# Streamed weights laid out page by page: 8 KB runs per partition instead of 1, 2 or 4 KB

## The chip, the cores and the metric

The kernel runs on one core of a Trainium2 chip. The metric is device time in microseconds (us) from one launch to its end, for the whole program. Lower is better. Laying out the inputs on the host is no part of the time.

## What is computed

Two transformer blocks run one after the other on 256 tokens of width 1024, with 256 context tokens beside them in the first block, in float32. The first block has two layers, the second has one. Every layer has the same shape, cut here to what matters:

```
mod   = silu(c) @ w_ada + b_ada                       # adaLN: w_ada is 1024 x 6144
h     = rms_norm(x) * (1 + scale1) + shift1
x     = x + gate1 * (mixer(h) @ w_out)                # w_out is 1024 x 1024
h2    = rms_norm(x) * (1 + scale2) + shift2
x     = x + gate2 * sum over 2 chosen experts of
          weight * ((silu(h2 @ w_gate[e]) * (h2 @ w_up[e])) @ w_down[e])
```

Layers 0 and 1 choose among 16 experts, whose three matrices are 1024 x 1024 each; layer 0 routes 512 tokens (latent and context), layer 1 routes 256. The third layer, called layer 2 below, chooses among 32 experts with matrices of 1024 x 256, 1024 x 256 and 256 x 1024. An expert's 12 MB (layers 0 and 1) or 3 MB (layer 2) are read from HBM once, so the experts stream 192, 192 and 96 MB.

## The kernel before

**Pages.** All large weights come into SBUF in pages of 1 MB, tiles of the tag `pg` with 8 KB in each of 128 partitions. A page is one DMA issued by SyncE (SP). `page()` takes a source seen as partition x k-tile x column and fetches it in two pages; `wpage()` hands out expert pages from several pools in turn: 8 page buffers in layer 0, 15 in layer 1 and 14 in layer 2. Some of these pools are opened while the mixer before them still runs, so that the first experts' pages are loaded ahead. A load can be issued when the last matmul that reads the old content of its buffer is done.

**Order.** The kernel is written in a tile framework that arranges the instructions on their engines and sets the semaphores; `gather` and `scatter` of other rounds are generators that `s.work()` advances between the matmuls of an expert.

**AdaLN.** `ada_chunk` (L234) multiplies the conditioning vectors with 512 columns of a 1024 x 6144 matrix: two pages, each partition of which holds four rows of 512 columns (2 KB each in HBM). The output projections of the three layers are loaded in the same form.

**Experts of layers 0 and 1.** `expert_wide` (from L1570) goes over the eight k-tiles in steps of two. For each step it loads one page of the gate and one of the up matrix, two k-tiles of 1024 columns each, so that a partition gets two rows of 4 KB that lie 512 KB apart. The matmuls of a k-tile (L1598, L1602) follow, then activation, transposes, and four pages of the down matrix in the same form (L1625, matmuls L1631 and L1635).

**Experts of layer 2.** `expert_narrow` (from L1645) serves two experts of 64 token slots, or four of 32, at a time, in column parts of the PE array. For gate and then up it loads one page an expert, eight rows of 256 columns (1 KB) in a partition (L1658, matmuls L1662), later one page an expert of the down matrix, two rows of 4 KB (L1681, matmuls L1686).

**Which expert.** The experts are visited in an order that depends on how many tokens chose them. `matrices(p)` reads the expert's index from SBUF into a register of SP, and `of_expert` takes a slice of each matrix at that register. `overflow` is a loop for tokens beyond the planned slots, run zero or more times.

**Already packed.** The first layer's input weights (`w0a`, `w0b`, `w0c`), layer 1's `w1` and the third layer's `w2b` are packed by the host, so that a page's partition is one run of 8 KB.

Of the kernel before, what the change touches and what calls it, by code (L numbers as in the profile page):

```python
# [20 lines left out]
P = 128  # L21
D = 1024
KT = 8
# [135 lines left out]
class K:  # L159
# [74 lines left out]
    def ada_chunk(self, ps, which, j, parts):  # L234

        nc, I = self.nc, self.I
        w = I["ada_w"][which] if which < 2 else I["w_ada_2"][0]
        s = 0 if which < 2 else 1
        wt = self.page(w[:, j * 512:(j + 1) * 512].rearrange("(k p) n -> p k n", p=P))
        pa = self.t(ps, [P, 512], "ad", bufs=1) if which == 2 and j >= 4 else self.t(ps, [P, 512], "mm")  # L240
        for kk in range(2):
            for g in range(4):
                k = g + 4 * kk
                nc.tensor.matmul(out=pa[32 * g:32 * g + 32, :], lhsT=self.st[:, s, k, :],
                                 rhs=wt[:, k, :], start=(kk == 0), stop=(kk == 1))
        pt = self.w2(parts, [P, 512]) if which == 2 and j >= 4 else self.t(parts, [P, 512], "part")
        (nc.scalar.copy if j % 2 else nc.vector.tensor_copy)(out=pt, in_=pa)  # L247
        return pt
# [428 lines left out]
    def mixer0(self):  # L677
        tc, nc, I = self.tc, self.nc, self.I
        with ExitStack() as st:
            A = self.pool(st, name="A", bufs=2, reuse_waits="tile")  # L680
            parts = self.pool(st, name="parts", bufs=3, reuse_waits="tile")
            ps = self.pool(st, name="psA", bufs=2, space=PSUM, reuse_waits="tile")
            self.vectors(ps, self.w2(A, [P, NVR, P]))
            x0 = []
            for i in range(4):
                x = self.w4(A, [P, D])
                nc.scalar.dma_start(out=x, in_=I["x" if i < 2 else "ctx"][0, (i % 2) * P:(i % 2 + 1) * P, :])
                x0.append(x)
            self.ada(ps, parts, 0, (1, 0))
            self.gain(0, 1, self.vc[:, V_NM0:V_NM0 + 8])  # L690
            acol, bcol = self.ac[0][:, 1], self.ac[0][:, 0]
            self.lower_bounds()
            hT = tuple(self.t(A, [P, KT, 512], f"hT{i}", F32R, bufs=1) for i in range(2))
            self.h_transposed(ps, A, hT, [(0, 0), (1, 0), (2, 1), (3, 1)], acol, bcol, x0)

            def weights(src):
                return self.split(A, self.page(src), "wh", 3)

            vt, dv = (self.t(A, [P, 4, 512], n, bufs=1) for n in ("vt", "dv"))
            w = weights(I["w0a"][0])  # L700
            self.hm = self.t(A, [P, 8, P], "hm", U8, bufs=1)
            hm = self.w4(A, [P, 1024])
            nc.sync.dma_start(out=hm, in_=I["cst2"][:, D_HM:D_HM + 1024])
            nc.vector.tensor_copy(self.hm.rearrange("p l t -> p (l t)"), hm)
            self.rope_tables(A)
            self.diff_lambda()
            for t in range(4):
                nc.scalar.copy(out=vt[:, t, :], in_=self.proj_tok(ps, hT, t, w, 0, 512))

            yT = Columns(self.xs)  # L710
            hg, df = {}, {}

            def dval(_=0):
                w = weights(I["w0a"][1])
                for t in range(4):
                    nc.scalar.copy(out=dv[:, t, :], in_=self.proj_tok(ps, hT, t, w, 0, 512))

            def H(h):
                if h not in hg:
                    hg[h] = self.hgrn_head(ps, A, hT, weights(I["w0b"][h]), h, vt, yT)  # L720
                next(hg[h])

            def F(h):
                if h not in df:
                    df[h] = self.diff_head(ps, A, hT, weights(I["w0c"][h]), 0, h, dv, yT)
                next(df[h])

            def a0(v):
                self.ada(ps, parts, 0, (v,))

            def a1(v):
                self.ada(ps, parts, 1, (v,))

            for f, v in ((H, 0), (H, 0), (H, 0), (H, 0), (a0, 2), (dval, 0), (F, 0), (F, 0), (H, 1), (F, 0), (H, 1), (H, 1), (H, 1), (a0, 4), (F, 1), (F, 1), (H, 2), (F, 1), (a1, 1), (H, 2), (H, 2), (H, 2), (a0, 3), (F, 2), (F, 2), (H, 3), (F, 2), (H, 3), (H, 3), (H, 3), (a0, 5), (F, 3), (F, 3), (a1, 0), (F, 3), (a1, 2)):
                f(v)
            self.ffn_gain(0)
            self.router_start(ps, A, 0)
            g1 = [self.as_row(ps, "lv", 0, 2, who, self.w4(A, [P, D])) for who in range(2)]
            x0 = []
            for i in range(4):  # L740
                x = self.w4(A, [P, D])
                nc.scalar.dma_start(out=x, in_=I["x" if i < 2 else "ctx"][0, (i % 2) * P:(i % 2 + 1) * P, :])
                x0.append(x)
            wo = []
            for half in range(2):
                w = self.page(I["even_w_out"][0][:, half * 512:(half + 1) * 512].rearrange("(k p) n -> p k n", p=P))
                wo.append(self.split(A, w, ("wh", "vt" if half else "wh"), (3, 1 if half else 3)))
            self.out_proj(ps, A, self.split_y(A, yT, ("hT0", "hT1")), wo, range(4), g1, 0, x0=x0)


    def mixer1(self):
        tc, nc, I = self.tc, self.nc, self.I
        with ExitStack() as st:
# [48 lines left out]
            g1 = [self.as_row(ps, "lv", 1, 2, 0, self.w4(A, [P, D]))]  # L802
            wo = []
            for half in range(2):
                w = self.page(I["w1o"][:, half * 512:(half + 1) * 512].rearrange("(k p) n -> p k n", p=P))
                wo.append(self.split(A, w, "wh", 4))
            self.out_proj(ps, A, self.split_y(Y, yT, ("y0", "y1")), wo, range(2), g1, 1, lambda: self.t(parts, [P, 512], "part"))

# [114 lines left out]
    def mixer2(self):  # L923
        tc, nc, I = self.tc, self.nc, self.I
        self.nw2, self.nw4 = 5, 3
        with ExitStack() as st:
# [55 lines left out]

            def wo():
                half = len(wos)
                w = self.page(I["w_out_2"][0][:, half * 512:(half + 1) * 512].rearrange("(k p) n -> p k n", p=P))
                wos.append(self.split(A, w, ("hT0", "hT1") if half else ("wh", "wh"), 1 if half else 2))

            todo = iter(ada[0:3] + [lru, None, None, *ada[3:4], lru, None, *ada[4:5], lru, *ada[5:], wo, wo])
# [581 lines left out]
    def expert_wide(self, s, src, x64, x32, s0):  # L1570
# [6 lines left out]
        for k2 in range(0, KT, 2):  # L1577
            if s.base is None:
                ws = [self.wpage([P, 2, D]) for _ in range(2)]
                for w, a in zip(ws, src):  # L1580
                    nc.sync.dma_start(out=w, in_=a[k2 * P:(k2 + 2) * P, :].rearrange("(k p) n -> p k n", p=P))
                rows = [[w[:, kk, :] for w in ws] for kk in range(2)]
            s.need(min(k2 + AHEAD, KT))
            for kk in range(2):
# [3 lines left out]
                else:  # L1588

                    w = self.wpage([P, 2, D])  # L1590
                    for i in range(2):
                        nc.sync.dma_start(out=w[:, i, :], in_=src[i][k * P:(k + 1) * P, :])
                    wk = [w[:, i, :] for i in range(2)]
                f = dict(start=(k == 0), stop=(k == KT - 1))
                for w, o in zip(wk, (pg, pu)) if x64 else ():
# [26 lines left out]
        p2 = self.t(ps, [P, 256], "py2", bufs=1) if x32 else None  # L1622
        for k2 in range(0, KT, 2):
            w = self.wpage([P, 2, D])
            nc.sync.dma_start(out=w, in_=src[2][k2 * P:(k2 + 2) * P, :].rearrange("(k p) n -> p k n", p=P))  # L1625
            for kk in range(2):
                g, b = divmod(k2 + kk, 4)
                f = dict(start=(k2 + kk == 0), stop=(k2 + kk == KT - 1))
# [16 lines left out]
    def expert_narrow(self, s, srcs, xT, c0, s0):  # L1645
# [8 lines left out]
        for i in range(2):  # L1654
            ws = []
            for src in srcs:
                w = self.wpage([P, KT, 256])
                nc.sync.dma_start(out=w, in_=src[i].rearrange("(k p) n -> p k n", p=P))  # L1658
                ws.append(w)
            for k in range(KT):  # L1660
                for e in range(ne):
# [16 lines left out]
        wd = []  # L1678
        for src in srcs:
            w = self.wpage([P, 2, D])  # L1680
            nc.sync.dma_start(out=w, in_=src[2].rearrange("(k p) n -> p k n", p=P))  # L1681
            wd.append(w)
        for h in range(2):
            for b in range(2):
# [11 lines left out]
    def moe(self, layer, plan, npages):  # L1696
# [6 lines left out]
        with ExitStack() as st:  # L1703
# [47 lines left out]
            if nt == 4:  # L1751
# [1 line left out]
                nc.vector.tensor_copy(s.ones, self.ones_b)  # L1753
                s.ds = self.t(G, [P, KT], "ds")
                self.tt(s.ds, self.ac[0][:, 3, :, 1], self.ac[0][:, 3, :, 0], ALU.subtract)
            if layer < 2:
                srcs = [I[n][layer] for n in ("moe_w_gate", "moe_w_up", "moe_w_down")]
            else:
                srcs = [I[n][0] for n in ("w_gate_2", "w_up_2", "w_down_2")]

            def matrices(p):

# [95 lines left out]

    @staticmethod
    def of_expert(srcs, e):  # L1860
        return [s_[bass.ds(e, 1)].rearrange("o d n -> (o d) n") for s_ in srcs]

    def overflow(self, s, G, slo, end, nbl, E, ob, srcs, xtile):

# [49 lines left out]
def prepare(inputs):  # L1914
# [16 lines left out]
    def pg(x):  # L1931
        return np.ascontiguousarray(x.transpose(1, 0, 2))

    q, ff, fb, i, g, dq, dk, dv = (w[:, :, j] for j in range(8))
    d["w0a"] = np.stack([pg(i), pg(dv)])
    d["w0b"] = np.stack([pg(np.concatenate([x[:, :, h * P:(h + 1) * P] for x in (q, ff, fb, g)], -1)) for h in range(4)])
    d["w0c"] = np.stack([pg(np.concatenate([x[:, :, h * P:(h + 1) * P] for x in (dq, dk)], -1)) for h in range(4)])
# [2 lines left out]
    w = a["odd_w_qkv"][0]  # L1940
    w = np.concatenate([w[:, :D][:, perm], w[:, D:]], 1).reshape(KT, P, 3, 512)
    d["w1"] = np.ascontiguousarray(w.transpose(2, 1, 0, 3))
    d["w1o"] = np.ascontiguousarray(a["odd_w_out"][0][perm])
    w = a["w_in_2"][0].reshape(KT, P, 1472)
    d["w2a"] = pg(w[:, :, :448])
    d["w2b"] = np.ascontiguousarray(w[:, :, 448:].reshape(KT, P, 2, 512).transpose(2, 1, 0, 3))
# [1 line left out]


_INS = ["x", "ctx", "vecs", "cst", "cst2", "w0a", "w0b", "w0c", "ada_w", "even_w_out", "diff_lambda",  # L1950
        "router_w", "router_b", "moe_w_gate", "moe_w_up", "moe_w_down",
        "final_norm_g", "swa_sink", "w1", "w1o", "w_ada_2", "positions_2", "w2a", "w2b", "q_norm_2", "k_norm_2", "w_q_b_2",
        "w_kv_b_2", "lru_wa_2", "lru_wx_2", "w_out_2", "w_router_group_2", "b_router_group_2", "w_router_expert_2",
        "b_router_expert_2", "w_gate_2", "w_up_2", "w_down_2"]


# [14 lines left out]
```

## Time and profile before

| what | value |
|---|---|
| median of 3 runs | 2214.55 us (2212.21 to 2215.14) |
| the profiled execution | 2221.57 us |
| its span, first to last instruction | 2219.7 us |
| mean granted TensorE clock | 0.962 of full speed |
| TensorE matmul busy | 1978.9 us, 89% of the span |
| VectorE, ScalarE, GpSimd busy | 42%, 25%, 11% |
| read from HBM | 629.51 MB, 284 GB/s over the span |
| loads of SP's and ScalarE's queues | 626.21 MB, 76.0% of the 16 DMA engines' span |

PE is TensorE's matmul, PEld its weight load, DVE VectorE, ACT ScalarE, POOL GpSimd, SPq the queue in which SyncE issues loads. L1598 is line 1598 of the kernel. A busy share is an average over stages with different limits, so it doesn't tell what bounds any one of them. The stages lie in the span about so: layer 0's mixer until 480, its experts until 1050, layer 1's mixer until 1310, its experts until 1780, layer 2's mixer until 1955, its experts until the end. "DMA share" is the summed time of all packets in a stretch over 16 engines' time; it can be a little above 1, since packets overlap.

### The profile page before, as it was taken

The page shows a single profiled execution, that of the slowest core. Times are in us where ns is not written, and L with a number is a line of the kernel's source. Part 1 is how long each engine was busy: PE and PEld are TensorE (multiplying, and loading weights), DVE is VectorE, ACT ScalarE, POOL GpSimd, SP SyncE. Part 2 cuts the span into 40 slices and gives each one's busy share as a digit, 9 for nine tenths or more (in the row PEclk, how much of TensorE's full clock was granted, in tenths as well). Part 3 has the DMA queues.
Part 4 walks back from the last instruction along what each step waited for, and adds up shares of the span by engine and source line. Part 5 has one row for each costly group of instructions (what it writes and reads, how often), then busy time and mean ns, then how long its engine had stood idle before and what let it go on. Part 6 is the DMA issues. An engine that isn't in the chain of part 4 may idle for free. (4 is left out here: it accounts for less than half of the span.)

```text
span 2219.7 us, 29536 instructions
## 1 busy us (share of the span) xinstructions
PE 1978.9 (89%) x11795; PEld 1023.2 (46%) x11795; DVE 940.9 (42%) x2121; ACT 549.9 (25%) x1010; POOL 248.2 (11%) x203
## 2 busy tenths in 40 slices
PE   6999999969999999999699989998877779989976
PEld 3766665755443434343555553332222255655422
DVE  4536546354443425242545543222211156556412
ACT  4333434232111111111433421101000055421100
POOL 0000000120111112031100000000000010113202
PEclk9999999989999999999799999999999989889988
DMA  8423426248999998998354669999999975779997
GB/s 306 157 77 133 146 83 227 76 146 298 346 378 375 360 345 333 351 374 336 105 176 156 237 252 410 409 409 409 409 409 409 410 252 205 267 257 365 360 371 277
DMA packets 238434, 632.58 MB, mean 285 GB/s; under 512 B 15440, under 2 KB 83024, under 8 KB 234960
## 3 DMA queue, kind: packets, MB, share of 16 engines
q1 hardware_dynamic: 236736, 626.21, 76.0%
q10 hardware_dynamic: 1552, 4.39, 0.5%
q8 instruction: 96, 1.57, 0.3%
q14 instruction: 50, 0.41, 0.1%
HBM read 629.51 MB, written 1.05 MB: 284 GB/s over the span
## 5 line engine op out<-in xcount | busy, mean ns | idle before, releaser
L1598 PE MATMUL gu<-pg,xT 128*64 128x512 f32 (+1 forms) x2560 | 489.0, 598 | 27.1 <-DMA pg<-in_moe_w_up_dram 14.6
L1631 PE MATMUL py<-pg,hT 128*64 128x512 f32 (+1 forms) x1280 | 258.5, 597 | 23.6 <-DVE hT L1615 17.4
L1598 PEld LDWEIGHTS gu<-pg,xT 128*64 128x64 f32 (+1 forms) x2560 | 132.5, 124 | 297.9 <-issue 227.7
L1567 POOL TENSOR_TENSOR xs<-xs,t 128x512 f32<-128x512 f32 x110 | 142.3, 1303 | 1121.8 <-DVE t L1222 1121.8
L1546 DVE SCALAR_TENSOR_TENSOR w<-py,swc,w 32x256 fp32r<-32x256 f32 (+3 forms) x142 | 95.5, 673 | 273.0 <-ACT w L1545 270.4
L375 PE MATMUL mm<-hT,wh 128*128 128x512 f32 (+1 forms) x672 | 193.6, 372 | 9.7 <-ACT w L431 5.1
L1545 ACT ACTIVATE w<-py,swc 32x256 fp32r<-32x256 f32 (+3 forms) x142 | 88.3, 622 | 409.7 <-PE py L1631 310.1
L1222 DVE TENSOR_TENSOR hid<-hid,gu 128x512 f32<-128x512 f32 (+2 forms) x52 | 32.8, 631 | 336.7 <-PE gu L1598 272.0
L1222 DVE TENSOR_TENSOR t<-x,w 128x512 f32<-128x512 f32 x156 | 105.7, 689 | 143.9 <-PE x L1563 124.2
L1631 PEld LDWEIGHTS py<-pg,hT 128*64 128x64 f32 (+1 forms) x1280 | 77.0, 124 | 137.4 <-issue 76.2
L375 PEld LDWEIGHTS mm<-hT,wh 128*128 128x128 f32 x672 | 120.3, 194 | 42.5 <-issue 8.9
L1563 PE MATMUL x<-w,S 128*128 128x512 f32 x312 | 112.9, 442 | 22.8 <-DVE t L1222 11.5
L1662 PE MATMUL gu<-pg,xT 128*32 128x256 f32 (+1 forms) x1024 | 109.2, 429 | 22.7 <-DMA pg<-in_w_up_dram 16.8
L375 PE MATMUL mm<-hT,pg 128*128 128x512 f32 (+1 forms) x336 | 124.1, 371 | 0.6 <-DVE pg L356 0.6
L1495 PEld LDWEIGHTS x<-oh,h 128*128 128x128 f32 x704 | 91.6, 189 | 55.8 <-issue 32.0
L1495 PE MATMUL x<-oh,h 128*128 128x256 f32 (+2 forms) x704 | 111.6, 292 | 5.4 <-DVE t L1222 2.4
L1608 ACT ACTIVATE hid<-gu 128x512 f32<-128x512 f32 (+1 forms) x41 | 24.4, 596 | 365.5 <-PE gu L1598 342.2
L1602 PE MATMUL gu<-pg,xT 128*32 128x512 f32 x640 | 111.6, 593 | 0.0
L1498 ACT ACTIVATE xT<-x,ac 128x256 f32<-128x256 f32 (+2 forms) x88 | 48.4, 550 | 211.8 <-PE x L1495 211.7
L1563 PEld LDWEIGHTS x<-w,S 128*128 128x128 f32 x312 | 49.2, 189 | 107.4 <-issue 32.7
L356 DVE TENSOR_TENSOR pg<-pg,wh 128x1024 fp32r<-128x1024 f32 (+1 forms) x74 | 89.0, 1210 | 20.4 <-ACT wh L355 20.3
L366 PE MATMUL mm<-wh,hT 128*128 128x512 f32 (+2 forms) x320 | 95.4, 378 | 2.1 <-ACT part L247 0.7
(500 smaller groups left out, 2621.1 us busy)
## 6 DMA issues: line engine op xcount, KB each, us to landing
pg<-in_moe_w_gate_dram SPq DMA_DIRECT2D x128, 1024.0 KB, 8.8
pg<-in_moe_w_up_dram SPq DMA_DIRECT2D x128, 1024.0 KB, 10.1
pg<-in_moe_w_down_dram SPq DMA_DIRECT2D x128, 1024.0 KB, 9.9
pg<-in_ada_w_dram SPq DMA_DIRECT2D x48, 1024.0 KB, 6.9
pg<-in_w_gate_dram SPq DMA_DIRECT2D x32, 1024.0 KB, 11.4
pg<-in_w_up_dram SPq DMA_DIRECT2D x32, 1024.0 KB, 11.8
pg<-in_w_down_dram SPq DMA_DIRECT2D x32, 1024.0 KB, 11.2
pg<-in_w_ada_dram SPq DMA_DIRECT2D x24, 1024.0 KB, 6.9
```

The source lines that it names most:

```text
L356: nc.vector.tensor_tensor(out=u[:, k:k + m], in0=x[:, k:k + m], in1=t[:, k:k + m].bitcast(F32), op=ALU.subtract)
L366: self.nc.tensor.matmul(out=pm, lhsT=hT[i][:, k, t * P:(t + 1) * P], rhs=w[j][:, k, c0:c0 + n], start=(m == 0), stop=(m == len(ops) - 1))
L375: self.nc.tensor.matmul(out=pm, lhsT=w[i][:, k, c0:c0 + P], rhs=hT[j][:, k, t0:t0 + nt], start=(m == 0), stop=(m == len(ops) - 1))
L1222: self.nc.vector.tensor_tensor(out=out, in0=a, in1=b, op=op)
L1495: nc.tensor.matmul(out=px[:, w, :], lhsT=l_, rhs=r_, start=(i == 0), stop=(i == len(ops) - 1))
L1546: nc.vector.scalar_tensor_tensor(out=lo[o:o + m, c0:c0 + w], in0=x, scalar=wc[o:o + m, :], in1=h.bitcast(F32), op0=ALU.mult, op1=ALU.subtract)
L1563: nc.tensor.matmul(out=px, lhsT=S[0:m, t * P:(t + 1) * P], rhs=y[0:m, cols], start=(i == 0), stop=(i == len(parts) - 1))
L1567: (nc.vector if last and h else nc.gpsimd).tensor_tensor(out=o, in0=o, in1=x, op=ALU.add)
L1598: nc.tensor.matmul(out=o[q:q + m64, :], lhsT=x64[0][:, k, x64[1] + r:x64[1] + r + m64], rhs=w[:, 512 * g:512 * g + 512], **f)
L1602: nc.tensor.matmul(out=pq[32 * q:32 * q + 32, :], lhsT=x32[0][:, k, x32[1]:x32[1] + 32], rhs=wk[q // 2][:, 512 * (q % 2):512 * (q % 2) + 5 ...
L1631: nc.tensor.matmul(out=py[q:q + m64, :], lhsT=h64[:, b, 64 * g + r:64 * g + r + m64], rhs=w[:, kk, 512 * h:512 * h + 512], **f)
L1662: nc.tensor.matmul(out=pg[r * e:r * e + r, 256 * i:256 * i + 256], lhsT=xT[:, k, c0 + r * e:c0 + r * e + r], rhs=ws[e][:, k, :], start=(k ...
```

## The change

The host writes every streamed matrix to HBM in the order in which the pages want it, so that the 8 KB of a partition are one contiguous run. The kernel's loads name the page instead of a strided view. Gate and up of an expert are stacked in one tensor, so that an expert has two source tensors instead of three. Buffers, sizes, the number of pages and all arithmetic stay as they are. In the overflow loop of layers 0 and 1 a page is still fetched in two loads of 4 KB rows.

```diff
@@ ada_chunk
-        w = I["ada_w"][which] if which < 2 else I["w_ada_2"][0]
+        w = I["ada_w"][which] if which < 2 else I["w_ada_2"]
-        wt = self.page(w[:, j * 512:(j + 1) * 512].rearrange("(k p) n -> p k n", p=P))
+        wt = self.page(w[j])
@@ output projections (the same in mixer1 and mixer2)
-                w = self.page(I["even_w_out"][0][:, half * 512:(half + 1) * 512].rearrange("(k p) n -> p k n", p=P))
+                w = self.page(I["even_w_out"][half])
@@ expert_wide
-                for w, a in zip(ws, src):
-                    nc.sync.dma_start(out=w, in_=a[k2 * P:(k2 + 2) * P, :].rearrange("(k p) n -> p k n", p=P))
+                for i, w in enumerate(ws):
+                    nc.sync.dma_start(out=w, in_=src[0][k2 // 2, i])
...
-                        nc.sync.dma_start(out=w[:, i, :], in_=src[i][k * P:(k + 1) * P, :])
+                        nc.sync.dma_start(out=w[:, i, :], in_=src[0][k // 2, i, :, k % 2, :])
...
-            nc.sync.dma_start(out=w, in_=src[2][k2 * P:(k2 + 2) * P, :].rearrange("(k p) n -> p k n", p=P))
+            nc.sync.dma_start(out=w, in_=src[1][k2 // 2])
@@ expert_narrow
-                nc.sync.dma_start(out=w, in_=src[i].rearrange("(k p) n -> p k n", p=P))
+                nc.sync.dma_start(out=w, in_=src[0][i])
...
-            nc.sync.dma_start(out=w, in_=src[2].rearrange("(k p) n -> p k n", p=P))
+            nc.sync.dma_start(out=w, in_=src[1])
@@ of_expert
-        return [s_[bass.ds(e, 1)].rearrange("o d n -> (o d) n") for s_ in srcs]
+        one = {6: "o a m p k n -> (o a) m p k n", 5: "o a p k n -> (o a) p k n", 4: "o p k n -> (o p) k n"}
+        return [s_[bass.ds(e, 1)].rearrange(one[len(s_.shape)]) for s_ in srcs]
@@ prepare, on the host
+    d["ada_w"], d["w_ada_2"] = cols(a["ada_w"], 512), cols(a["w_ada_2"][0], 512)
+    d["even_w_out"], d["w_out_2"] = cols(a["even_w_out"][0], 512), cols(a["w_out_2"][0], 512)
+    d["moe_gu"] = np.stack([pairs(a["moe_w_gate"]), pairs(a["moe_w_up"])], 3)
+    d["moe_d"] = np.ascontiguousarray(pairs(a["moe_w_down"]))
+    d["moe2_gu"] = np.stack([a[n][0].reshape(32, KT, P, 256).transpose(0, 2, 1, 3) for n in ("w_gate_2", "w_up_2")], 1)
+    d["moe2_d"] = np.ascontiguousarray(a["w_down_2"][0].reshape(32, 2, P, D).transpose(0, 2, 1, 3))
...
-    d["w1o"] = np.ascontiguousarray(a["odd_w_out"][0][perm])
+    d["w1o"] = cols(a["odd_w_out"][0][perm], 512)
```

`cols(x, n)` puts a matrix's column blocks of n in front, then partition, k-tile and column; `pairs(x)` puts pairs of k-tiles in front, then partition, the two k-tiles and the columns.

## Rows read from the trace of the kernel before

**Rows 1.** The page: busy shares, GB/s in 40 equal slices, DMA packets.

```profile
PE 1978.9 (89%) x11795; PEld 1023.2 (46%) x11795; DVE 940.9 (42%) x2121; ACT 549.9 (25%) x1010; POOL 248.2 (11%) x203
...
GB/s 306 157 77 133 146 83 227 76 146 298 346 378 375 360 345 333 351 374 336 105 176 156 237 252 410 409 409 409 409 409 409 410 252 205 267 257 365 360 371 277
DMA packets 238434, 632.58 MB, mean 285 GB/s; under 512 B 15440, under 2 KB 83024, under 8 KB 234960
```

**Rows 2.** Busy time by stretches; the first line names the columns.

```profile
core 0: us, PE busy (x) PEld busy (x) DVE busy (x) ACT busy (x) POOL busy (x), PEclk, DMA share, GB/s
10.00:30.00 20.00, 13.76 (x68) 3.17 (x68) 5.97 (x19) 4.42 (x9) 1.65 (x3) 1.00 1.05 388
30.00:35.00 5.00, 2.66 (x20) 1.43 (x20) 0.51 (x3) 1.33 (x3) 0.00 (x0) 1.00 1.04 427
31.00:35.00 4.00, 2.66 (x20) 1.43 (x20) 0.51 (x3) 1.33 (x3) 0.00 (x0) 1.00 1.01 422
540.00:1040.00 500.00, 487.37 (x3690) 195.05 (x3690) 199.82 (x361) 80.58 (x142) 92.75 (x71) 1.00 0.95 362
1344.00:1776.00 432.00, 367.81 (x1616) 118.38 (x1614) 86.76 (x159) 34.53 (x54) 36.26 (x28) 1.00 1.03 409
1957.00:2046.00 89.00, 88.60 (x608) 52.75 (x609) 45.66 (x122) 17.93 (x31) 17.79 (x14) 1.00 0.95 322
2046.00:2204.00 158.00, 128.66 (x956) 54.80 (x956) 53.94 (x108) 15.44 (x27) 32.19 (x25) 0.91 1.05 365
2046.00:2100.00 54.00, 50.92 (x417) 25.34 (x414) 29.26 (x61) 8.62 (x15) 16.73 (x13) 1.00 1.07 365
2100.00:2204.00 104.00, 77.73 (x541) 29.46 (x543) 24.68 (x47) 6.82 (x12) 15.47 (x13) 0.87 1.04 364
```

**Rows 3.** PE's waits, 0 to 45: us in total, times, longest.

```profile
PE mm L244 <- DMA pg<-in_ada_w_dram: 10.6, 6, 6.2
```

**Rows 4.** PE's waits for loads, 1490 to 1790.

```profile
PE gu L1598 <- DMA pg<-in_moe_w_up_dram: 14.6, 24, 0.6
PE gu L1598 <- DMA pg<-in_moe_w_gate_dram: 12.5, 21, 0.7
...
PE py L1631 <- DMA pg<-in_moe_w_down_dram: 5.5, 7, 1.9
```

**Rows 5.** PE's waits for loads, 2100 to 2205.

```profile
PE gu L1662 <- DMA pg<-in_w_up_dram: 16.8, 9, 2.5
PE gu L1662 <- DMA pg<-in_w_gate_dram: 5.9, 4, 2.4
PE py L1686 <- DMA pg<-in_w_down_dram: 1.4, 2, 0.7
```

**Rows 6.** PE's waits, 540 to 1040: the longest entry.

```profile
PE py L1631 <- DVE hT L1615: 5.4, 7, 0.8
```

**Rows 7.** SP's issues in time, 1386 to 1402: start, duration, load.

```profile
1391.85 2.45 SPq L1581 DMA_DIRECT2D pg<-in_moe_w_up_dram  x1
...
1396.98 2.31 SPq L1581 DMA_DIRECT2D pg<-in_moe_w_up_dram  x1
```

**Rows 8.** SP's issues in time, 572 to 592.

```profile
584.54 0.37 SPq L1581 DMA_DIRECT2D pg<-in_moe_w_gate_dram  x1
```

**Rows 9.** The page's list of loads: count, KB each, median us to landing.

```profile
pg<-in_moe_w_gate_dram SPq DMA_DIRECT2D x128, 1024.0 KB, 8.8
...
pg<-in_w_gate_dram SPq DMA_DIRECT2D x32, 1024.0 KB, 11.4
...
pg<-in_w0a_dram SPq DMA_DIRECT2D x4, 1024.0 KB, 8.5
```

**Rows 10.** SP's issues in time, 1254 to 1260.5.

```profile
1254.73 0.37 SPq L1581 DMA_DIRECT2D pg<-in_moe_w_gate_dram  x1
1259.16 0.37 SPq L1625 DMA_DIRECT2D pg<-in_moe_w_down_dram  x1
1259.58 0.50 SPq L1581 DMA_DIRECT2D pg<-in_moe_w_up_dram  x1
```

More of the change, by code (lines that the diff above doesn't have):

```diff
@@ L804, in mixer1 @@
             for half in range(2):
-                w = self.page(I["w1o"][:, half * 512:(half + 1) * 512].rearrange("(k p) n -> p k n", p=P))
+                w = self.page(I["w1o"][half])
                 wo.append(self.split(A, w, "wh", 4))
@@ L984, in wo @@
                 half = len(wos)
-                w = self.page(I["w_out_2"][0][:, half * 512:(half + 1) * 512].rearrange("(k p) n -> p k n", p=P))
+                w = self.page(I["w_out_2"][half])
                 wos.append(self.split(A, w, ("hT0", "hT1") if half else ("wh", "wh"), 1 if half else 2))
@@ L1755, in moe @@
                 self.tt(s.ds, self.ac[0][:, 3, :, 1], self.ac[0][:, 3, :, 0], ALU.subtract)
[L1756 to L1759, printed above, removed]
+            srcs = [I[n][layer] for n in ("moe_gu", "moe_d")] if layer < 2 else [I[n] for n in ("moe2_gu", "moe2_d")]
             def matrices(p):
@@ L1934, in prepare, with cols, pairs @@
     q, ff, fb, i, g, dq, dk, dv = (w[:, :, j] for j in range(8))
+    def cols(x, n):
+        x = x.reshape(*x.shape[:-2], KT, P, x.shape[-1] // n, n)
+        return np.ascontiguousarray(np.moveaxis(x, (-2, -3, -4), (-4, -3, -2)))
+    def pairs(x):
+        x = x.reshape(*x.shape[:-2], x.shape[-2] // (2 * P), 2, P, x.shape[-1])
+        return np.moveaxis(x, -2, -3)
+    d["ada_w"], d["w_ada_2"] = cols(a["ada_w"], 512), cols(a["w_ada_2"][0], 512)
[4 more added lines that the diff above has]
+    d["moe2_d"] = np.ascontiguousarray(a["w_down_2"][0].reshape(32, 2, P, D).transpose(0, 2, 1, 3))
     d["w0a"] = np.stack([pg(i), pg(dv)])
@@ L1950 @@
 _INS = ["x", "ctx", "vecs", "cst", "cst2", "w0a", "w0b", "w0c", "ada_w", "even_w_out", "diff_lambda",
-        "router_w", "router_b", "moe_w_gate", "moe_w_up", "moe_w_down",
+        "router_w", "router_b", "moe_gu", "moe_d",
         "final_norm_g", "swa_sink", "w1", "w1o", "w_ada_2", "positions_2", "w2a", "w2b", "q_norm_2", "k_norm_2", "w_q_b_2",
         "w_kv_b_2", "lru_wa_2", "lru_wx_2", "w_out_2", "w_router_group_2", "b_router_group_2", "w_router_expert_2",
-        "b_router_expert_2", "w_gate_2", "w_up_2", "w_down_2"]
+        "b_router_expert_2", "moe2_gu", "moe2_d"]
 def kernel(**inputs):
```

## Prediction

> **What bounds the kernel now.** I read the page first, then stretches of it, then PE's waits, then the queue that issues the loads. On the page TensorE (PE) is busy for 89% of the span, so the kernel looks PE-bound as a whole; but the row of GB/s is not level, and one run of eight slices stands at 409 to 410 without a break [rows 1]. A stream that holds one value for 444 us (eight slices of 55.5 us) is at its own limit, whatever the average says. So the question is asked stage by stage [rows 2]:
>
> - Start, 10 to 30: DMA share 1.05 and 388 GB/s, PE busy 13.8 of 20 us. These are layer 0's adaLN weights, in runs of 2 KB. The stream bounds.
> - Layer 0's experts, 540 to 1040: PE 487.4 of 500 us. PE bounds.
> - Layer 1's experts, 1344 to 1776: 409 GB/s, PE 367.8 of 432 us. The stream bounds.
> - Layer 2's experts: until 2046 PE 88.6 of 89 us, then 128.7 of 158 us at 365 GB/s. First PE bounds, then the stream.
>
> PE's waits say the same from the other side. It waits for adaLN pages for 10.6 us within the first 45 us [rows 3], for layer 1's pages for 14.6 + 12.5 + 5.5 = 32.6 us, all after 1490 [rows 4], and for layer 2's for 16.8 + 5.9 + 1.4 = 24.1 us, all after 2100 [rows 5]. The list over the whole span holds no other wait of PE for a load than the small vectors at the start. In layer 0's list no load appears at all; the longest entry is 5.4 us on VectorE [rows 6].
>
> The issuing queue tells full from starved. In layer 1 one issue after the other takes 2.3 to 2.5 us: the queue behind it is full, and that is about the time of one 1 MB page at 409 GB/s (2.56 us) [rows 7]. In layer 0 an issue takes 0.37 us and comes when PE gives a page free [rows 8].
>
> **The change part by part.**
>
> *Number of loads.* Every page stays 1 MB and keeps its one issue, on SP, into the same buffer: as many issues as before, of 1024 KB each [rows 9]. Bytes are unchanged. No engine gets or loses an instruction. SP works out two run-time base addresses an expert instead of three; SP is not on the path (it waits for PE or for the queue), so I take nothing. The overflow loop, the only place where a page still comes in two loads of 4 KB runs, isn't entered: the 128 gate pages are 32 experts at 4 each [rows 9]. The host's rearranging is outside the time.
>
> *Run length.* This is all there is. A partition's 8 KB now come from one run instead of two of 4 KB (layers 0 and 1, layer 2's down matrices), four of 2 KB (adaLN and output projections), or eight of 1 KB (layer 2's gate and up). What a run length is worth is read from saturated stretches of this trace: 365 GB/s where two thirds of the bytes come in 1 KB runs, 388 at 2 KB, 409 at 4 KB [rows 2]. The packed weights of the first layer are already in 8 KB runs (the w0a row of [rows 9]), and the one stretch in which they alone fill the queues, 31 to 35 us, shows 422 GB/s at a share of 1.01 [rows 2]. It is short, and a few smaller packets are in it. So I take 422, with 409 (the longer run brings nothing over 4 KB) and 427 (the same pages with the us before them, 30 to 35) as bounds.
>
> *Start.* 20 us at 388 become 20 x 388/422 = 18.4: 1.6 us, since PE waits there and everything follows from these vectors. Bounds 1.0 and 1.8.
>
> *Layer 0 experts and the mixers.* Nothing. The work that hides the loads is PE's own: 487.4 busy of 500 us, and the idle 12.6 are waits on VectorE and ScalarE [rows 2, 6]. Were that cover gone, layer 0's stream would be the end, and it too would be faster than before.
>
> *Layer 1 experts.* 432 x (1 - 409/422) = 13.3 us. It needs waits of PE that can go: 32.6 us are there, so the stream stays the bound and PE goes on waiting, some 19 us. That PE's waits begin only at 1490 while the queue is full from about 1344 does not halve this: in between PE eats up pages loaded ahead, and a faster stream makes that stock last longer. Bounds 0 and 432 x (1 - 409/427) = 18.2.
>
> *Layer 2 experts.* 158 x (1 - 365/422) = 21.3 us, against 24.1 us of waits that can go: nearly all of PE's waiting, so PE and the stream would end almost together. Bounds 158 x (1 - 365/409) = 17.0 and, PE allowing no more, 24.1. The granted clock of 0.87 after 2100 [rows 2] should rise towards 1.00 as the gaps close; I take nothing for it, because the stream then sets the end.
>
> *Sum.* 1.6 + 13.3 + 21.3 = 36.2 us. The profiled execution took 2221.57 us (span 2219.7, 1.9 around it), which is 7.0 above the median of the runs. Without the 36.2 it is 2185.4, and the median goes from 2214.55 to 2178.4 us.
>
> [...]
>
> **The rivals.**
>
> 1. *4 KB is already the top.* The stream gains in layer 2 and at the start, not in layer 1: 17.0 + 1.0 = 18.0 us, 2196.5 us. For it: the 422 rests on 4 us of trace. Against it: those 4 us have a share of 1.01, so they aren't flattered by an idle queue.
> 2. *PE takes over early in layer 2.* From 2046 to 2100 PE is busy 50.9 of 54 us [rows 2]; if pages that come sooner find no free buffer there, only the stretch from 2100 counts: 104 x (1 - 364/422) = 14.3 in place of 21.3, in all 29.2, 2185.3 us. Against it: the queue is full there (share 1.07), so buffers are being given free in time.
> 3. *The runs don't become long.* The experts are addressed by a number known only at run time; if such a load were still cut into its inner rows, layers 1 and 2 would keep 4 KB and 1 KB packets, and a ceiling that run length doesn't move gives the same. 2214.6 us, or 1.6 less for the start. For it: no load with a run-time address in this trace has a whole-page run to show. Against: in memory such a page is as contiguous as w0a's, whose address is fixed.
> 4. *Slower: another order of instructions.* The order on the queues isn't that of the code: a down page of layer 1 goes out between a gate and an up page, which the code issues after all of these [rows 10]. So the order is arranged when the program is built, and cheaper loads may change it. The place where it would hurt is layer 0, where PE has no slack. The price: to end over 2219 it must eat the 36.2 and 4.4 us more, 40.6 over 16 experts, a new wait of 2.5 us in each, which is three times the 0.8 us of the longest single wait on VectorE in layer 0's list now [rows 6]. Below that point the change is still faster.
>
> **How the numbers follow.** Forecast 0.65; rival 1 0.12; rival 2 0.13; rival 3 0.05; rival 4 0.05. I give the forecast that much because both halves of it, the present rate and the future one, are read from the same trace, and PE's waits are large enough to pay it. The time is that of the forecast, 2178 us. Its upper rate gives 1.8 + 18.2 + 24.1 = 44.1 us, 2170.4; rival 1 gives 2196.5. The range from 2170 to 2196 holds the forecast, rival 2 and about half of rival 1, some 0.84; it leaves out rivals 3 and 4. What a measurement of this kernel can tell from no change is 0.2%, 4.4 us. Faster by more than that: 0.65 + 0.12 + 0.13 = 0.90. Within it: rival 3, 0.05. Slower: rival 4, 0.05.
>
> **What would show each step.** The packets: 480 expert pages, 72 of adaLN and 12 of output projections make 564 x 128 = 72,192 packets of 8 KB, in place of 215,040 smaller ones (384 x 256 + 64 x 1024 + 32 x 256 + 84 x 512); the total falls from 238,434 [rows 1] to about 95,600. If it stays near 200,000, rival 3 holds. Layer 1's level row of GB/s should read about 422 instead of 409 and be 13 us shorter; 409 again is rival 1. PE's waits for layer 1's loads should fall from 32.6 to about 19 us, layer 2's from 24.1 to about 3. Layer 0's stretch should keep its length within 2 us; if it is longer by tens of us, with waits that aren't in the old list, rival 4 holds. I am wrong if the gain lies outside these three stretches, or if pages arrive sooner and the end doesn't move.

## The result and the profile after

The changed kernel takes 2178.23 us (median of 4 runs, 2176.03 to 2183.1), against 2214.85 us for the kernel before, run beside it: a ratio of 0.9838 [0.9823, 0.9852], so 36.6 us faster, with an interval of 32.8 to 39.2. The prediction was 2178 us. The profiled execution took 2183.1 us, its span 2181.3.

The page of the changed kernel, as in [rows 1]; the last two lines are from its list of loads, as in [rows 9]:

```profile
PE 1961.6 (90%) x11795; PEld 1018.2 (47%) x11795; DVE 941.4 (43%) x2121; ACT 550.1 (25%) x1010; POOL 247.1 (11%) x203
...
GB/s 315 153 80 135 145 87 232 78 116 289 348 377 374 369 363 346 316 362 404 126 150 172 177 258 367 421 421 420 421 421 421 421 283 239 253 243 376 397 420 303
...
DMA packets 95586, 632.58 MB, mean 290 GB/s; under 512 B 15440, under 2 KB 17488, under 8 KB 19920
...
pg<-in_moe_gu_dram SPq DMA_DIRECT2D x320, 1024.0 KB, 9.3
pg<-in_moe_d_dram SPq DMA_DIRECT2D x160, 1024.0 KB, 9.8
```

Instructions, loads and bytes are as many as before; the packets fell from 238,434 to 95,586. The level run of slices, 409 to 410 before, is at 420 to 421; it fills seven slices of 54.5 us, where it filled eight of 55.5. (Layer 2's pages are counted with the others: 256 + 64 and 128 + 32.)

The stretches of [rows 2], moved by what the kernel had gained up to each:

```profile
core 0: us, PE busy (x) PEld busy (x) DVE busy (x) ACT busy (x) POOL busy (x), PEclk, DMA share, GB/s
10.00:30.00 20.00, 12.13 (x68) 3.06 (x68) 6.39 (x21) 6.16 (x12) 2.21 (x4) 1.00 1.02 422
537.00:1037.00 500.00, 487.35 (x3692) 195.17 (x3690) 199.80 (x361) 80.41 (x141) 92.71 (x72) 1.00 0.93 362
1341.00:1761.00 420.00, 366.16 (x1618) 119.86 (x1616) 87.03 (x159) 34.62 (x55) 36.23 (x28) 1.00 1.01 421
1939.00:2028.00 89.00, 88.60 (x606) 52.82 (x608) 45.75 (x122) 18.10 (x32) 17.77 (x14) 1.00 0.87 337
2028.00:2166.00 138.00, 120.22 (x962) 53.20 (x961) 53.94 (x109) 15.44 (x27) 32.44 (x25) 0.95 0.99 408
2028.00:2081.00 53.00, 50.07 (x418) 24.67 (x415) 29.20 (x62) 8.62 (x15) 16.42 (x13) 1.00 1.00 407
2081.00:2166.00 85.00, 70.15 (x546) 28.53 (x547) 24.74 (x47) 6.82 (x12) 16.02 (x13) 0.92 0.98 408
```

Layer 0's stretch holds the same work in the same 500 us. Layer 1's stretch does the same matmuls (1,616 and 1,618 are counted) in 420 instead of 432 us, layer 2's second stretch (956 and 962) in 138 instead of 158. The last two lines cut that stretch where [rows 2] cut it at 2100: 53 instead of 54 us come before the cut, 85 instead of 104 behind it. So 19 of the 20 us are won at the end, though the stream is faster (407 instead of 365 GB/s) from the start: until the cut PE is the bound, and what comes sooner is kept in the buffers and spent later.

PE's waits for loads in layer 1 (1480 to 1790), as in [rows 4]:

```profile
PE gu L1598 <- DMA pg<-in_moe_gu_dram: 18.6, 34, 0.7
...
PE py L1631 <- DMA pg<-in_moe_d_dram: 3.9, 7, 1.5
```

in layer 2 (2080 to 2180), as in [rows 5]:

```profile
PE gu L1662 <- DMA pg<-in_moe_gu_dram: 11.0, 7, 1.9
PE py L1686 <- DMA pg<-in_moe_d_dram: 1.8, 3, 0.6
```

and at the start (0 to 45), as in [rows 3]:

```profile
PE mm L244 <- DMA pg<-in_ada_w_dram: 8.1, 5, 2.5
```

32.6 us became 22.5 in layer 1, 24.1 became 12.8 in layer 2, 10.6 became 8.1 at the start.

Where each layer's experts begin and end can be read to a tenth of a us: from the start of the layer's first routing matmul (L1345) to the start of its last scatter matmul (L1563), and in layer 2 to the end of the last instruction that counts as busy, 5 us before the end of the span. A mixer is what lies between. In us, from the profiled executions (four of the experiments told below have columns as well):

| stage | before | after | layer 0 alone | layer 1 alone | layer 2 alone | adaLN alone |
|---|---|---|---|---|---|---|
| mixer 0, with the start | 472.9 | 469.7 | 468.6 | 465.7 | 468.7 | 467.9 |
| experts 0 | 592.6 | 592.9 | 592.8 | 593.4 | 593.5 | 592.7 |
| mixer 1 | 237.6 | 237.7 | 237.2 | 237.7 | 237.6 | 238.1 |
| experts 1 | 479.3 | 467.1 | 478.5 | 466.7 | 478.6 | 478.8 |
| mixer 2 | 167.1 | 164.3 | 164.2 | 161.5 | 164.0 | 162.6 |
| experts 2 | 265.2 | 244.5 | 265.1 | 265.1 | 245.7 | 265.1 |

The experts' stages repeat within 1.2 us in this table wherever their layout is the same. Mixers 0 and 2 don't: they wander over 7 and 6 us in kernels that leave them untouched, with the same matmuls in the same order, and their granted clock lies below 1 (0.95 before and 0.96 after in the last 290 us of mixer 0). In the twelve profiled executions of whole kernels mixer 2's length goes with that clock: 166.8 to 167.1 us at a mean of 0.87, 162.7 to 164.3 at 0.88 to 0.89, 161.4 to 162.6 at 0.90. What one profiled execution gains there says nothing of the change.

### The profile page after: what moved, and what is told of

It is laid out like the page before. It is cut to its first block, busy times and chain, and to the rows that moved or that the text cites. A ratio compares the mean times of both kernels' runs of the same rounds, so it can differ in the third digit from the quotient of the medians.

```text
span 2181.3 us, 29536 instructions
## 1 busy us (share of the span) xinstructions
PE 1961.6 (90%) x11795; PEld 1018.2 (47%) x11795; DVE 941.4 (43%) x2121; ACT 550.1 (25%) x1010; POOL 247.1 (11%) x203
## 2 busy tenths in 40 slices
DMA packets 95586, 632.58 MB, mean 290 GB/s; under 512 B 15440, under 2 KB 17488, under 8 KB 19920
## 5 line engine op out<-in xcount | busy, mean ns | idle before, releaser
L375 PE MATMUL mm<-hT,wh 128*128 128x512 f32 (+1 forms) x672 | 189.1, 365 | 10.0 <-ACT w L431 5.1
L1222 DVE TENSOR_TENSOR hid<-hid,gu 128x512 f32<-128x512 f32 (+2 forms) x52 | 32.8, 632 | 306.5 <-PE gu L1598 261.7
L1563 PE MATMUL x<-w,S 128*128 128x512 f32 x312 | 114.9, 450 | 21.3 <-DVE t L1222 10.1
L1662 PE MATMUL gu<-pg,xT 128*32 128x256 f32 (+1 forms) x1024 | 101.2, 401 | 11.0 <-DMA pg<-in_moe_gu_dram 11.0
L1563 PEld LDWEIGHTS x<-w,S 128*128 128x128 f32 x312 | 50.4, 192 | 106.5 <-issue 31.7
```

The source lines that it names most:

```text
L375: self.nc.tensor.matmul(out=pm, lhsT=w[i][:, k, c0:c0 + P], rhs=hT[j][:, k, t0:t0 + nt], start=(m == 0), stop=(m == len(ops) - 1))
L1222: self.nc.vector.tensor_tensor(out=out, in0=a, in1=b, op=op)
L1563: nc.tensor.matmul(out=px, lhsT=S[0:m, t * P:(t + 1) * P], rhs=y[0:m, cols], start=(i == 0), stop=(i == len(parts) - 1))
L1662: nc.tensor.matmul(out=pg[r * e:r * e + r, 256 * i:256 * i + 256], lhsT=xT[:, k, c0 + r * e:c0 + r * e + r], rhs=ws[e][:, k, :], start=(k ...
```

## The experiments

**Each part alone.** Four kernels put one part of the new layout into the kernel before. Each edit is the part of the change's diff that bears on its layer; layers left alone keep the old views:

```diff
-                srcs = [I[n][layer] for n in ("moe_w_gate", "moe_w_up", "moe_w_down")]
...
+                srcs = [I["gu1"], I["d1"]]
...
-                    nc.sync.dma_start(out=w, in_=a[k2 * P:(k2 + 2) * P, :].rearrange("(k p) n -> p k n", p=P))
...
+                    nc.sync.dma_start(out=w, in_=src[0][k2 // 2, i] if len(src) == 2 else
+                                      src[i][k2 * P:(k2 + 2) * P, :].rearrange("(k p) n -> p k n", p=P))
```

(layer 1; for layers 0 and 2 the same with their tensors; for adaLN and the output projections only the edits in `ada_chunk` and the mixers).

> Only layer 0's experts are packed in 8 KB runs; all else as before. My theory (run length sets the rate of the stream, and the time follows only where PE waits for it): no change beyond 2 us, about 2214.8 us, because PE has no wait for a load in that stretch. Rival (faster loads help wherever there are loads, for instance through fewer packets beside PE's own reads): a third to two fifths of the gain, 13 us or more, since these are 192 of the 564 MB repacked.

Measured: 2215.72 us, ratio 1.0003 [0.9992, 1.0013], experts 0 592.8 us against 592.6. The packets fell to 213,858 and the time stood still: layer 0's loads are covered.

> Only layer 1's experts are packed. My theory: 432 us at 409 GB/s become 432 x 409/421, 12.3 us less, about 2202.5 us, with PE's waits for layer 1's loads down from 32.6 to about 22 us. Rival (the gain of layer 1 depends on what came before or after it): clearly less than 10 or more than 15 us.

Measured: 2200.22 us, 0.9936 [0.9921, 0.995]; experts 1 12.6 us shorter, the level at 420 to 421 GB/s. PE's waits for layer 1's loads in this kernel (1470 to 1780):

```profile
PE gu L1599 <- DMA pg<-in_gu_dram: 19.0, 34, 1.0
...
PE py L1633 <- DMA pg<-in_d_dram: 3.4, 7, 1.3
```

That is 22.4 us, against 22.5 in the whole change. Rival 1, that 4 KB is already the top, falls here.

> Only layer 2's experts are packed. My theory: 158 us at 365 GB/s become 158 x 365/421, 21 us less, about 2194 us. Rival (PE is the bound until 2100 and only the rest counts): 14 us less, 2201 us.

Measured: 2191.5 us, 0.9889 [0.9874, 0.9903]; experts 2 19.5 us shorter. That is far nearer the forecast's 21.3 than rival 2's 14.3. As shown above for the whole change, the stretch from 2046 to 2100 gains hardly any time itself; the pages that come sooner in it find free buffers, and the time is won after it.

> Only the adaLN weights and the output projections are packed. My theory: 1.5 us at the start and nothing elsewhere, about 2213.3 us. Rival (the mixers gain from earlier pages as well, as the two traces seem to say: 1.7 us in layer 0's mixer and 2.4 in layer 2's): 5.6 us less, 2209 us. If the rival is wrong, those 4 us come from the granted clock, which differs from run to run.

Measured: 2212.61 us, 0.9996 [0.9983, 1.0009]: a gain of 1.5 us can't be seen in totals. The 5.6 us of the rival, a ratio of 0.9975, lie outside the interval, so the shorter mixers of the first pair can't all be the change's doing. The 1.5 us can be seen in the trace. The first transposing matmul of L327 comes when the first adaLN vectors are there; its line in the kernel before, and after it in this one (the last numbers are first and last start):

```profile
L327 PE MATMUL tp<-cst,w x80: 271/421/478, 33.6 to 1798.3; 128*128 128x128 f32 x80
```

```profile
L327 PE MATMUL tp<-cst,w x80: 271/421/477, 31.6 to 1793.4; 128*128 128x128 f32 x80
```

In the four kernels with 2 KB adaLN runs (before and the three experiments above) it starts at 33.6 to 34.0 us, in the changed kernel, this one and the six further variants of the changed kernel at 31.6 to 32.1. The two groups don't touch.

The four ratios add up to -1.76%, 39 us, against 36.6 for the whole: the parts are additive within their intervals.

**The loads by themselves.** This kernel streams weights in six run lengths, one after the other:

```diff
+            for j in range(4):
+                nc.sync.dma_start(out=part(w, j, 2048).rearrange("p (k n) -> p k n", n=256), in_=mb(g, 4 * i + j, 1).rearrange("(k p n) -> p k n", p=P, n=256))
...
+            for j in range(4):
+                nc.sync.dma_start(out=part(w, j, 2048), in_=mb(g, 4 * i + j, 1).rearrange("(p n) -> p n", p=P))
...
+            nc.sync.dma_start(out=w, in_=mb(u, 4 * i, 4).rearrange("(p n) -> p n", p=P))
```

> Leaves out all of the computation: it only loads 24 MB each in runs of 1, 2, 4, 8 and 16 KB and 8 MB in runs of 32 KB, from contiguous pages, one after the other, with full queues, and returns no result of the model. My theory: a packet costs a fixed time and its bytes at one rate, so with 4 KB at 409 and 1 KB at about 349 GB/s the fixed part is about 9.5 ns and the rate 27.35 bytes per ns and engine: 349, 389, 411, 424, 431 and 434 GB/s. Rival (8 KB is the end of it): 16 and 32 KB stay at 421 to 424. Second rival (the rates in the kernel are set by what runs beside the loads): 1, 2 and 4 KB are well above 350, 389 and 411 when nothing else runs.

Its stretches of 1, 2, 4, 8, 16 and 32 KB, in this order:

```profile
core 0: us, DVE busy (x) POOL busy (x), PEclk, DMA share, GB/s
20.00:60.00 40.00, 2.00 (x13) 0.00 (x0) 1.00 1.10 348
90.00:130.00 40.00, 2.15 (x14) 0.00 (x0) 1.00 1.05 387
150.00:190.00 40.00, 2.40 (x16) 0.00 (x0) 1.00 1.03 410
210.00:245.00 35.00, 2.21 (x15) 0.00 (x0) 1.00 1.01 422
265.00:300.00 35.00, 1.50 (x14) 0.00 (x0) 1.00 1.00 427
320.00:330.00 10.00, 0.21 (x2) 0.00 (x0) 1.00 1.00 431
```

388, 409 and 422, which the prediction read between other work, come back within 1 GB/s on an idle core. So what runs beside the loads doesn't set the level (the second rival), and run length does: from 1 to 8 KB a load is 1 MB throughout. The rates go on rising, to 427 and 431, so the first rival falls too, though the loads of 16 and 32 KB runs are also larger (2 and 4 MB) and the last line rests on 10 us. All six are within 4 GB/s of what was expected. Every megabyte lies contiguous in HBM here, as layer 1's and layer 2's pages did before: that doesn't help as long as a partition's share of it is cut up.

**A run length given back.** The changed kernel, with layer 2's gate and up pages in four runs of 2 KB:

```diff
-                nc.sync.dma_start(out=w, in_=src[0][i])
+                nc.sync.dma_start(out=w.rearrange("p (a k) n -> p a (k n)", a=4), in_=src[0][i].rearrange("a p k n -> p a (k n)"))
...
```

> The changed kernel, but layer 2's gate and up pages come in 2 KB runs (four in a partition); each page is still one contiguous megabyte. My theory: the 57.7 MB from 2046 on go at 2/3 of 389 and 1/3 of 421, about 399 GB/s, in 144.5 in place of 137 us: 7 us slower than the changed kernel, about 2185.5 us. Rival (that a page is packed and contiguous counts, not the run): as the changed kernel, 2178 us.

Measured: 2184.08 us, 0.9868 [0.9845, 0.989]; experts 2 250.1 us, 5.6 longer than in the changed kernel (244.5), where 7 were expected. The two kernels differ in the 64 x 128 x 3 = 24,576 packets that are added (120,163 in all) and in nothing else.

**Only the place in HBM.** Layer 1's 8 KB runs stay, but lie 64 KB (gate and up) or 32 KB (down) apart instead of one behind the other:

```diff
-                    nc.sync.dma_start(out=w, in_=src[0][k2 // 2, i])
+                    nc.sync.dma_start(out=w, in_=src[0][:, k2 // 2, i] if s.layer == 1 else src[0][k2 // 2, i])
...
+    d["moe_gu1"] = np.ascontiguousarray(gu[1].transpose(0, 3, 1, 2, 4, 5))
+    d["moe_d1"] = np.ascontiguousarray(dn[1].transpose(0, 2, 1, 3, 4))
```

> The changed kernel, but layer 1's 8 KB runs of one page lie 64 KB apart (down matrix 32 KB) instead of one behind the other. My theory: the run is what counts, so the time stays at 2178 us within 3 us, 421 GB/s in layer 1. Rival (the gain came from a page being one contiguous megabyte): layer 1 falls back to 409 or below, 2190 us or more. The pages of before were contiguous as well in the experts, which speaks against the rival already.

Measured: 2183.6 us, 0.9849 [0.9828, 0.9871]; experts 1 467.2 us against 467.1, the level at 420 to 421. At these distances the pages needn't be contiguous. (The median is 5 us above that of the changed kernel, and the intervals of the two ratios overlap. In the profiled execution, at 2188.85 us the slowest of the four, the part that was changed has none of the excess; mixers 0 and 2 took 471.7 and 167.0 us, the upper end of their wander.)

**Longer runs still.** Layer 1's gate and up as one load of 2 MB in 16 KB runs, with the same 15 MB of buffers (four of 2 MB, seven of 1 MB):

```diff
-                ws = [self.wpage([P, 2, D]) for _ in range(2)]
-                for i, w in enumerate(ws):
-                    nc.sync.dma_start(out=w, in_=src[0][k2 // 2, i])
+                if self.pairs:
+                    w = self.wpair()
+                    nc.sync.dma_start(out=w, in_=src[0][k2 // 2])
+                    ws = [w[:, 0], w[:, 1]]
...
```

> The changed kernel, but in layer 1 a gate and an up page are one load of 2 MB with 16 KB runs, in 4 buffers of 2 MB and 7 of 1 MB instead of 15 of 1 MB. My theory: two thirds of the bytes at about 429 and a third at 421, 426 GB/s instead of 421: 417 us become 412, 5 us less than the changed kernel, about 2173 us. Rival (coarser buffers make PE wait): no gain or a loss, 2178 us or more.

Measured: 2187.24 us, 0.9877 [0.9859, 0.9896]; experts 1 471.1 us, 4.0 longer than in the changed kernel; where the rest of the 9 us between the medians lies isn't shown. The rate did rise, to 424 to 427. But at the start of the stage, where PE eats what was loaded ahead, the queue runs dry. Two stretches of this kernel:

```profile
core 0: us, PE busy (x) PEld busy (x) DVE busy (x) ACT busy (x) POOL busy (x), PEclk, DMA share, GB/s
1320.00:1340.00 20.00, 20.00 (x104) 9.06 (x102) 5.17 (x14) 3.59 (x7) 0.00 (x0) 1.00 0.82 347
1340.00:1360.00 20.00, 20.00 (x94) 6.66 (x92) 5.79 (x16) 1.97 (x4) 0.00 (x0) 1.00 0.87 340
```

and the same of the changed kernel, whose stage begins 1.5 us later:

```profile
1320.00:1340.00 20.00, 20.00 (x103) 8.75 (x99) 5.76 (x15) 4.39 (x8) 0.00 (x0) 1.00 0.98 399
1340.00:1360.00 20.00, 20.00 (x93) 7.13 (x94) 7.10 (x21) 2.91 (x5) 0.00 (x0) 1.00 1.01 420
```

In these 40 us 20 x (52 + 80) KB/us = 2.6 MB fewer came in, 6.3 us at 420 GB/s. The higher rate wins back less than half of that (from 1440 to 1700 it is 425 instead of 421 GB/s, 2.4 us). A buffer of 2 MB comes free only when its last k-tile is used, and it is for such a buffer that SP waits before it issues, in the same 40 us of this kernel and of the changed one:

```profile
SPq L1581 <- PE gu L1603: 29.9, 6, 12.7
```

```profile
SPq L1581 <- PE gu L1598: 14.6, 6, 5.1
```

The variant also ties gate and up to 8 MB of the buffers and down to 7, where any page could take any buffer before; no run tells this from the size of the buffers. No variant here beats the changed kernel.

**How good layer 0's cover is.** The changed kernel with layer 0's pages in shorter runs, of 1 KB and of 2 KB (then n=512):

```diff
+                    if s.layer == 0:
+                        nc.sync.dma_start(out=w.rearrange("p a (b n) -> p (a b) n", n=256), in_=src[0][k2 // 2, i].rearrange("a p n -> p a n"))
...
```

> The changed kernel, but layer 0's pages come in 1 KB runs. My theory: layer 0 draws 362 GB/s and PE bounds it; 1 KB runs give 348 at most, so the stream becomes the bound there: 500 x 362/348 = 520, up to 20 us more in layer 0's stretch, with new waits of PE for loads in it; 2193 to 2198 us. Rival (layer 0 is covered whatever the loads do): no change, 2178 us.

Measured: 2191.15 us, 0.9895 [0.9879, 0.9912]; experts 0 604.5 us, 11.6 longer. The page's row of GB/s, whose slices 11 to 19 now stand level:

```profile
GB/s 314 154 78 135 144 88 230 78 140 293 348 348 348 348 347 348 347 347 348 191 154 162 184 269 356 422 421 420 421 421 421 422 277 240 235 246 378 401 420 299
```

Two waits of PE for loads are new (467 to 1071, where the changed kernel's list has none):

```profile
PE py L1641 <- DMA pg<-in_moe_d_dram: 1.7, 1, 1.7
PE gu L1605 <- DMA pg<-in_moe_gu_dram: 1.5, 7, 0.2
```

They make 3.2 of the 11.6 us. Another 8.8 show as busy time: PE's in the stage went from 571.45 to 580.22 us, with equal counts and a granted clock of 0.99 in both. The weight loads (PEld) tell more. They have waits for pages of layer 0 as well, where the changed kernel's list for the stage has none:

```profile
PEld gu L1605 <- DMA pg<-in_moe_gu_dram: 12.1, 18, 1.2
PEld py L1641 <- DMA pg<-in_moe_d_dram: 3.1, 2, 2.5
```

These 15.2 us are enough for the 11.6. In this stage PE is busy for 580.22 and PEld for 240.28 of 604.5 us, so weight loads and matmuls overlap, and part of such a wait can lie under matmuls that still count as busy. That the 8.8 us come from there fits these numbers, but no line shows it.

> The changed kernel, but layer 0's pages come in 2 KB runs. My theory: 387 GB/s are still more than the 362 that PE takes, so layer 0's stretch keeps its length within 2 us and PE gets no wait for a load; 2178 us. Rival (the cover thins gradually, because PE's demand comes in bursts): 3 to 10 us more.

Measured: 2179.64 us, 0.9851 [0.9834, 0.9867]; experts 0 592.6 us. PE's and PEld's lists for the stage have no wait for a load. At 387 GB/s the cover is whole, at 348 it is not; PE draws 362 there.

**Layer 1 below the old level.** The changed kernel with layer 1 in 2 KB runs, by the same edit with `s.layer == 1` and n=512:

> The changed kernel, but layer 1's pages come in 2 KB runs. My theory: 177 MB at 387 instead of 421 GB/s take 457 instead of 420 us: 37 us more in layer 1's stretch, 2215 us, which is 24 us more there than with the 4 KB runs of before. Rival (the stretch has a second bound near 409): less than 15 us more.

Measured: 2217.57 us, 1.0018 [1.0002, 1.0034]; experts 1 505.3 us, 38.2 longer than in the changed kernel and 26.0 longer than before. The level is 386 to 387, and PE's waits for layer 1's loads over the whole span are

```profile
PE gu L1605 <- DMA pg<-in_moe_gu_dram: 41.6, 57, 1.0
...
PE py L1641 <- DMA pg<-in_moe_d_dram: 10.2, 19, 1.6
```

51.8 us against 22.5. One layer's run length, two steps shorter, eats up the whole change.

## Why the prediction was right, step by step

- **Start: 1.6 forecast, 1.5 measured** (33.6 to 32.1 in the profiled pair, 1.5 to 2.4 between the two groups of kernels). Over the whole span PE's waits for adaLN pages only fell from 10.6 to 9.8 us in the profiled pair, and the totals can't tell 1.5 us, so that these reach the end isn't shown.
- **Layer 0 and the mixers: 0 forecast, 0 shown.** The experts' stage is 0.3 us longer, and alone it gave 1.0003. The named cover is what hides it, PE's own work, which draws less than the stream can give: 1 KB runs, which give less than PE draws (348 against 362 GB/s), cost 11.6 us.
- **Layer 1: 13.3 forecast, 12.2 measured** (479.3 to 467.1 us; 12.6 alone). The term is off by its rate: the level is 421, not the 422 of the short w0a stretch, and 432 x (1 - 409/421) = 12.3. The waits kept 22.5 us, not 19: 10.1 us of waiting went, and PE's busy time over the stretch fell by 1.7 us as well.
- **Layer 2: 21.3 forecast, 20.7 measured** (19.5 alone). The mechanism held, but that the size comes so near is partly luck. The stretch ran at 408 GB/s, not 422, and by that rate the term is 158 x (1 - 365/408) = 16.7 us. The other 3.3 of its 20.0 us were won ahead of it: over the 89 us before, the stream brought 337 GB/s instead of 322 [rows 2], 1.3 MB that no longer had to come. One sentence was wrong: that nearly all of PE's waiting would go. 12.8 us stayed, because PE's own work got shorter: over the second stretch it was busy 120.2 instead of 128.7 us, at a granted clock of 0.95 instead of 0.91 [rows 2]. 8.4 us less work and 11.3 us less waiting make 19.7 of the 20.0 by which the stretch shrank. The clock rose as the prediction said, and the gain isn't larger for it since the stream sets the end. Rival 2 was right that PE is the bound until 2100, and wrong that the faster stream is lost there: 19 us, not 14.3, were won after it.
- **The sum: 36.2 forecast, 36.6 measured** in medians. The stages of the profiled pair give 1.5 + 12.2 + 20.7 = 34.4; the profiled execution's own 38.5 has about 4 us of the mixers' wander in it. So that forecast and medians meet within 0.4 us is luck; what the record bears is some 34 us from the named stages, and an interval of 32.8 to 39.2 for the whole.
- **Rival 3** fell with the packets, 95,586 against 95,600 foretold: a page addressed by a register is cut in 8 KB packets as one with a fixed address is (packets of 8 KB or more went from 238,434 - 234,960 = 3,474 to 95,586 - 19,920 = 75,666: 72,192 more, 128 for each of the 480 expert pages and of the 84 with fixed addresses). **Rival 4** fell too: the instructions of PE, ScalarE and GpSimd and SP's loads stand in the same order as before, VectorE's but for two pairs of neighbours that swapped.
- **A ceiling that run length doesn't move**, the other half of rival 3, isn't borne out: with nothing else on the core 1 KB runs reach 348 GB/s and 8 KB runs 422, and the 1 KB layout cost 11.6 us in layer 0.

## What to carry to other kernels

Look for slices of the GB/s row that stand level: in this kernel the stream was at the limit of its run length there, and a longer run was worth length x (1 - old rate / new rate), 12.3 us by the sum and 12.2 by the trace in layer 1. A stretch in which PE still bounds isn't lost for this: the pages that come sooner wait in free buffers and pay later, as in layer 2, where 19 of the 20 us were won behind it. Where PE bounds, compare what it draws with the rate of the run length; layer 0's 362 GB/s were safe at 387 and not at 348. Longer runs were worth having here until they needed coarser buffers: 16 KB runs won 3 to 6 GB/s, and the stage was 4 us longer for a queue that ran dry.

## What the runs showed that I had not expected

**A fixed price per packet.** The prediction read each rate by itself; the loads alone put them on one line. If every run is one packet (for 1 to 8 KB the packet counts of the two kernels fit that) and the 16 engines share them evenly, a packet of 1 KB takes an engine 16 x 1024 / 348 = 47.1 ns, one of 4 KB 16 x 4096 / 410 = 159.8: an estimate of 9.5 ns each and 27.2 bytes per ns. By that line 2 and 8 KB give 387 and 423 GB/s (387 and 422 measured), 16 and 32 KB 429 and 432 (427 and 431).

**The queue.** Before, an issue in layer 1 held SP for 2.3 to 2.5 us [rows 7]. With 8 KB runs each takes 0.33 us (from 1386 to 1480):

```profile
L1581 SPq DMA_DIRECT2D pg<-in_moe_gu_dram x27: 327/328/328, 1386.3 to 1477.7; - x27
```

and SP's longest waits in that stretch are now for an earlier page to land:

```profile
SPq L1581 <- DMA pg<-in_moe_d_dram: 24.2, 12, 2.2
SPq L1625 <- DMA pg<-in_moe_gu_dram: 22.7, 12, 2.1
SPq L1581 <- DMA pg<-in_moe_gu_dram: 21.6, 12, 2.2
```

That long issues go with many packets in the queue fits both kernels (256 packets a page before, 128 after), but no run here measured the queue's depth, and none shows that it changed the time. So the prediction's sign that a queue is full, the long issue, isn't a general one: layer 1's stream is at its limit in both kernels, with issues of 2.3 to 2.5 us in one and of 0.33 us in the other.
